# Turning attention probabilities outside TensorE in a two-layer diffusion backbone: VectorE 32x32 blocks and a round trip through DRAM

## The chip, the cores and the metric

The kernel runs on one core of one Trainium2 chip. The metric is the device time of one execution in microseconds. The kernel before took 809.46 us (median of 3 runs, 809.27 to 809.84). A difference of less than about 0.2% can't be told from no change.

A core has TensorE (PE in the profile; PEld are its weight loads), VectorE (DVE), ScalarE (ACT), GpSimd (POOL) and SyncE (SP), which here only issues DMAs.

## The reference

512 latent tokens and 256 context tokens of width 1024 pass two layers. Layer 0 is differential attention (8 heads, each with two score maps over head width 64), layer 1 grouped-query attention (8 query heads of width 128 on 2 key/value heads). Latent queries read all 768 keys, context queries (layer 0 only) read the 256 context keys.

```python
h = rms_norm(x, pre_g[i]) * (1 + scale) + shift        # scale, shift, gate from adaLN of c
q, k, v, z = split(h @ w_in)                           # layer 1: q, k also RMS-normed; then rotary
s = einsum('bqhgd,bkhd->bhgqk', q, k) * Dh ** -0.5
p = softmax(s, axis=-1)
o = einsum('bhgqk,bkhd->bqhgd', p, v)
# layer 0:  o = o1 - lam * o2, rms_norm(o, subln_g) * (1 - lam_init)
y = (o * silu(z)) @ w_out
x = x + gate * rms_norm(y, post_g[i])
```

Everything is float32; the kernel splits each operand of a large product in a rounded part and a rest (`hi` and `lo`) and adds three products (`mm3`: hi·hi, hi·lo, lo·hi).

## The kernel before

Tokens stand in tiles of 128. In layer 0 the kernel goes head by head; a head has three chunks: chunk 0 and 1 are two query tiles each of latent tokens (256 queries against 768 keys), chunk 2 the two query tiles of context. Layer 1 has 8 heads with two chunks of two latent query tiles. A **pair** is such a chunk of 256 latent queries of one head: 16 in layer 0, 16 in layer 1, 32 in all.

A pair passes these steps. One score unit for each of its two query tiles (`s_units`, `s1_units`): TensorE writes scores into the PSUM tile `sc`, VectorE takes the row maximum (`tensor_reduce`), ScalarE the exponential into `p`, GpSimd scales `p` by the reciprocal sum; in layer 0 VectorE then subtracts the second map (`scalar_tensor_tensor`). Now `p` holds queries on partitions, but the product with v needs keys on partitions. So a `tstep` for each 256 keys lets TensorE transpose four 128x128 blocks into a PSUM bank (12 transposes in a pair), ScalarE copies them, rounded, to `ah`, VectorE forms the rest `al`. An `mstep` then multiplies with v: six matmuls of 256 columns, 18 in a pair (tiles `bk<-ah,vh` and the like).

Between these steps TensorE does the projections (q, k, v, the gate z) and the output products of the layer; those that aren't due are "fill". Weights come by one queue: SP loads a 512 KB block into `raw` (2 buffers), ScalarE rounds it to `whi`, GpSimd or VectorE forms `wlo`; 3 or 4 such pairs of tiles are held.

The order of all instructions on every engine, SP's DMA issues too, is fixed when the program is built: class `Plan` records each operation with a price and a priority, `Plan.schedule` lays them out in time with these prices, and the result is written to the engines in this order. An engine works in that order and waits at each instruction for what it needs; whatever stands behind it on this engine waits too. The lines of all these operations are one line of the profile (L395 before, L411 after), so tiles are told apart by name.

Of the kernel before, what the change touches and what calls it, by code (L numbers as in the profile page):

```python
# [15 lines left out]
P = 128  # L16
# [31 lines left out]
WBUFS = 3  # L48
XE = [2, 2, 2, 2, 3, 3]
# [24 lines left out]
AB = 3  # L74
MEM = 227168
AHEAD_OPS = 1500
MARGIN = 1.08
SLOT = {}
# [28 lines left out]
class Plan:  # L107


    def __init__(self, mem, psum, sizes):  # L110
        self.mem, self.sizes = mem, sizes
# [10 lines left out]
    def pool(self, name, side="left", psum=False):  # L122
        return Pool(self, name, side, psum)

# [41 lines left out]
    def add(self, q, meth, args, kw):  # L166
# [14 lines left out]
        for aps_, w in ((ins, 0), (outs, 1)):  # L181
            for ap in aps_:
                if ap.space == bass.MemoryType.DRAM:
                    continue
                name, spans, parts = self.places(ap)
                if name not in self.banks:
# [103 lines left out]
    def schedule(self, rank):  # L290
# [15 lines left out]
        while len(order) < count:  # L306
# [79 lines left out]
class Emit:  # L386
# [7 lines left out]
    def add(self, eng, meth, args, kw):  # L394
        self.ops.append(getattr(eng, meth)(*args, **kw))  # L395
        return self.ops[-1]

# [81 lines left out]
def tile_backbone(  # L479
# [30 lines left out]
    ps1 = ctx.enter_context(pl.pool("ps1", psum=True))  # L510

# [24 lines left out]

    def mm3(o, ahi, alo, bhi, blo, start, stop):
# [4 lines left out]
    def pv_mm(o, vh, vl, c, ah, al, kt, first, last):  # L542
        terms = [(v, a, e) for v, a in ((vh, ah), (vl, ah), (vh, al)) for e in range(2)]
        for i, (v, a, e) in enumerate(terms):
            nc.tensor.matmul(o, v[:, kt + e, c], a[:, e * 256:e * 256 + 256], start=first and i == 0, stop=last and i == 5)
# [492 lines left out]
    def v_mm(o, w, t, k_lo=0, k_hi=KT, first=True, last=True):  # L1038
        for kt in range(k_lo, k_hi):
            sl = slice(t * P, (t + 1) * P)  # L1040
# [82 lines left out]
    with pl.pool("t0") as t0:  # L1123
# [58 lines left out]
        def qk_split_(h, rr, eng=nc.gpsimd):  # L1182
            qk[h] = tuple(t0.tile([P, T], F32R, tag=f"qk{i}", name=nm("qk"), bufs=1) for i in range(4))
            for r, hi, lo in ((rr[0], *qk[h][:2]), (rr[1], *qk[h][2:])):
# [79 lines left out]
        def s_units(h, qts):  # L1264
            res = []

            def unit(qt):
# [11 lines left out]
                prev = None  # L1279
                for j in range(nk // w):  # L1280
                    c = slice(k0 + j * w, k0 + j * w + w)
                    for i, (a, b) in enumerate(((qh, kh_), (qh, kl_), (ql, kh_))):
                        for m in (1, 0):
                            r = slice(m * 64, m * 64 + 64)
                            with after(prev), chained(prev):
                                prev = nc.tensor.matmul(
                                    sc[m][:, j if nk == T else m, :w], a[r, tok], b[r, c], start=i == 0, stop=i == 2)
                for m in range(2):
# [3 lines left out]
                    pt = t0.tile([P, T], F32, tag=f"p{m}", name=nm("p"), bufs=6 if m == 0 else 2)[:, :nk]  # L1292
# [827 lines left out]
```

## Time and profile before

| | before |
|---|---|
| median of 3 runs | 809.46 us |
| the profiled execution: its own time | 808.79 us |
| its span | 807.0 us |
| mean granted TensorE clock | 0.993 |
| busy: PE / PEld | 786.4 us (97%) / 699.8 us (87%) |
| busy: DVE / ACT / POOL | 473.6 (59%) / 482.0 (60%) / 437.4 us (54%) |
| moved by DMA | 77.78 MB, mean 96 GB/s |

The span is the time from the first to the last instruction. A matmul's busy time runs longer than the step from one matmul to the next, since matmuls are pipelined; where the rate of TensorE matters, the starts of neighbours are to be read. The DMA columns of a window are the mean busy share of the core's 16 DMA engines and the rate in GB/s.

### The profile page before, as it was taken

What the parts mean: (1) busy time and instruction counts of PE and PEld (TensorE: products, weight loads), DVE (VectorE), ACT (ScalarE), POOL (GpSimd) and SP (SyncE); (2) the same over time, 40 slices, a digit from 0 to 9 for tenths busy, and PEclk for the clock granted to TensorE, in tenths of its full rate; (3) what the DMA queues carried; (4) which work ended last, traced back from release to release, by engine and by line L of the source; (5) the groups of instructions that cost most, each with busy time, mean ns of one, the idle gap of its engine ahead of it and who ended that gap; (6) DMA issues with size and microseconds to landing.
All of it is one profiled execution on the core that took longest, in us unless ns stands there. A gap on an engine that the chain in (4) does not pass through costs nothing.

```text
span 807.0 us, 14385 instructions
## 1 busy us (share of the span) xinstructions
PE 786.4 (97%) x5482; PEld 699.8 (87%) x5482; DVE 473.6 (59%) x824; ACT 482.0 (60%) x1083; POOL 437.4 (54%) x512
## 2 busy tenths in 40 slices
PE   7899999999999999999999999999999999999997
PEld 5779888889887898797989998898999899898886
DVE  3425787774847546656546743788346455655625
ACT  5524577684565645666538843784466676768622
POOL 4545776874585654757923312366887646644101
PEclk9899999999999999999999999999999999999999
DMA  9951120132142431323430152035321200201112
GB/s 302 363 180 67 65 75 31 40 108 89 40 158 79 144 105 53 105 80 96 165 106 27 62 227 79 1 89 175 120 70 53 96 11 27 79 27 55 51 53 105
DMA packets 41541, 77.78 MB, mean 96 GB/s; under 512 B 3584, under 2 KB 18688, under 8 KB 41472
## 3 DMA queue, kind: packets, MB, share of 16 engines
q1 hardware_dynamic: 38048, 71.71, 27.4%
q10 hardware_dynamic: 3424, 5.15, 1.8%
q8 instruction: 43, 0.70, 0.4%
q14 instruction: 26, 0.21, 0.1%
HBM read 70.56 MB, written 2.10 MB: 90 GB/s over the span
## 4 chain that ended last, share of the span: by engine, by line
PE 91%; DVE 3%; ACT 2%; DMA 2%; issue 1%; SPq 0%; POOL 0%; ACTq 0%; DVEq 0%; POOLq 0%
PE bk L395 75%; PE sc L395 16%; DMA ag<-in_ada_w 1%; DMA raw<-in_post_g 1%; DVE gacc L395 1%; DMA gw<-in_ada_w 0%; ACT whi L395 0%; SPq L395 0%; DVE h L395 0%; ACT sq L395 0%; DVE hf L395 0%; ACT p L395 0%; DVE sw L395 0%; DVE gate L395 0%; ACT jk L395 0%
## 5 line engine op out<-in xcount | busy, mean ns | idle before, releaser
L395 PE MATMUL bk<-whi,h 128*128 128x256 f32 (+1 forms) x1184 | 244.6, 299 | 2.0 <-DVE kn L395 1.3
L395 PE MATMUL bk<-h,whi 128*128 128x512 f32 (+2 forms) x832 | 225.6, 351 | 0.0
L395 POOL TENSOR_TENSOR wlo<-raw,whi 128x256 fp32r<-128x256 f32 x200 | 162.5, 839 | 76.7 <-ACT whi L395 75.3
L395 PEld LDWEIGHTS bk<-whi,h 128*128 128x128 f32 x1184 | 191.0, 189 | 14.6 <-issue 4.9
L395 PE MATMUL bk<-wlo,h 128*128 128x256 f32 (+1 forms) x592 | 176.5, 299 | 0.0
L395 PEld LDWEIGHTS bk<-h,whi 128*128 128x128 f32 x832 | 144.1, 188 | 16.5 <-issue 4.4
L395 PE MATMUL bk<-h,wlo 128*128 128x512 f32 (+2 forms) x416 | 145.7, 351 | 0.0
L395 DVE TENSOR_REDUCE sm<-sc 128x1 f32<-128x768 f32 (+2 forms) x114 | 101.0, 897 | 25.7 <-PE sc L395 25.4
L395 PEld LDWEIGHTS bk<-wlo,h 128*128 128x128 f32 x592 | 111.7, 189 | 4.8 <-issue 1.4
L395 POOL TENSOR_SCALAR p<-p,sm 128x768 f32<-128x768 f32 (+1 forms) x80 | 68.4, 858 | 77.6 <-DVE sm L395 72.8
L395 DVE TENSOR_TENSOR al<-bk,ah 128x512 fp32r<-128x512 f32 x104 | 69.4, 685 | 39.3 <-ACT ah L395 38.8
L395 ACT CAST whi<-raw 128x1024 fp32r<-128x1024 f32 (+1 forms) x70 | 71.7, 1026 | 31.9 <-PE bk L395 27.7
L395 ACT ACTIVATE p<-sc,sm 128x768 f32<-128x768 f32 (+1 forms) x96 | 72.9, 762 | 21.6 <-DVE sm L395 15.6
L395 ACT CAST ah<-bk 128x512 fp32r<-128x512 f32 x104 | 59.0, 590 | 43.5 <-PE bk L395 43.1
L395 PEld LDWEIGHTS bk<-h,wlo 128*128 128x128 f32 x416 | 78.4, 188 | 7.5 <-issue 1.3
L395 PE MATMUL bk<-ident,p 128*128 128x128 f32 x416 | 64.3, 275 | 1.6 <-DVE ql L395 1.1
L395 PEld LDWEIGHTS bk<-ident,p 128*128 128x128 f32 x416 | 49.0, 141 | 11.4 <-issue 2.0
L395 DVE SCALAR_TENSOR_TENSOR p<-p,sm,p 128x768 f32<-128x768 f32 (+1 forms) x48 | 53.4, 1120 | 3.3 <-POOL p L395 0.5
L395 ACT ACTIVATE jk<-bk 128x128 f32<-128x128 f32 (+4 forms) x66 | 22.7, 345 | 53.5 <-PE bk L395 34.4
L395 POOL TENSOR_TENSOR sz<-sz,za 128x384 f32<-128x384 f32 (+1 forms) x24 | 29.4, 1227 | 40.3 <-ACT za L395 39.7
L395 PE MATMUL sc<-qk,qk 64*128 64x384 f32 (+1 forms) x480 | 50.6, 341 | 0.0
L395 DVE RECIPROCAL sm<-sm 128x1 f32<-128x1 f32 (+1 forms) x114 | 18.1, 159 | 52.0 <-ACT p L395 51.5
(191 smaller groups left out, 1375.5 us busy)
## 6 DMA issues: line engine op xcount, KB each, us to landing
raw<-in_a_w SPq DMA_DIRECT2D x30, 512.0 KB, 3.5
araw<-in_ada_w SPq DMA_DIRECT2D x12, 1024.0 KB, 5.3
raw<-in_b_w SPq DMA_DIRECT2D x20, 512.0 KB, 3.5
ag<-in_ada_w SPq DMA_DIRECT2D x32, 256.0 KB, 6.5
raw<-in_w_out SPq DMA_DIRECT2D x16, 512.0 KB, 3.6
sw<-qr ACTq DMA_DIRECT2D x32, 128.0 KB, 2.1
gw<-in_ada_w SPq DMA_DIRECT2D x8, 512.0 KB, 4.1
xt<-in_x SPq DMA_DIRECT2D x4, 512.0 KB, 5.1
```

The costliest lines, as they stand in the source:

```text
L395: self.ops.append(getattr(eng, meth)(*args, **kw))
```

## The change

A pair's latent probabilities are no longer transposed by TensorE. The exponentials of both query tiles go into one tile `pp` of 24 x 2 x 32 columns: 24 blocks of 32 keys, and in each the two query tiles side by side. When both are scaled, `turn` lets VectorE transpose all 32x32 blocks of `pp` in place in one instruction (128 x 1536). SP then stores `pp` to two DRAM scratch tiles `dr` (64 partitions of 1536 floats each, 384 KB) and reads them back with four loads of 192 KB into `at` (128 partitions x 4 x 384). Store and loads stand in SP's one queue; a load waits for the landing of its half store. ScalarE and VectorE split `ah` and `al` straight from `at` in SBUF instead of from a PSUM bank. The 32 transposes of the context chunks stay on TensorE.

The blocks come back with the keys in another order, so this order is given to keys and values: the score products read permuted k tiles (`ordered`, `k_tr`), and the v projections read their 128 tokens of h with a step of 4 tokens (latent tiles) or 2 (context tiles) as TensorE's weights (`keys`). The buffers of `ah` and `al` go from 3 to 2 (`AB`), the six (layer 0) or five (layer 1) single `p` tiles give way to two `pp` and two `at`. In the plan every DMA is taken to land 1000 ns later (`DPAD`), and SP's issue is priced at 450 ns instead of 330; so the order on all engines is laid out anew.

```diff
+DPAD = 1000
...
-AB = 3
...
+AB = 2
+P0B = 2
+ATB = 2
+PPB = 2
+DRSPLIT = 2
+DRB = 6
+PEWAY = ((), ())
...
-                go = s + (330 if e == "SP" else 450)
+                go = s + 450
                 dma = max(dma, go + 300) + op.cost / 350.0
-                end = max(go + 1700 + op.cost / 350.0, dma) + (800 if op.cost == 131072 else 300)
+                end = max(go + 1700 + op.cost / 350.0, dma) + (800 if op.cost == 131072 else 300) + DPAD
...
+    def keys(src, t):
+        if t < NQ:
+            return src[:, :S].rearrange("p (x k) -> p k x", k=4)[:, t]
+        return src[:, S:].rearrange("p (x k) -> p k x", k=2)[:, t - NQ]
...
+    def by_k(ap, n):
+        return by_a(ap, 192)[:, :, P:].rearrange("p a (k j) -> p k a j", k=2) if n == 2 else ap.rearrange("p (a k j) -> p k a j", a=4, k=6)
...
+    def turn(pool, pp):
+        flat = pp.rearrange("p b u x -> p (b u x)")
+        nc.vector.transpose(flat, flat)
+        at = pool.tile([P, 4, 384], F32, tag="at", name=nm("at"), bufs=ATB)
+        for lo in range(0, 4, 4 // DRSPLIT):
+            n = 4 // DRSPLIT
+            dr = drp.tile([P // DRSPLIT, 4 * 384], F32, tag="dr", name=nm("dr"), bufs=DRB)
+            nc.sync.dma_start(dr[:, :], flat[32 * lo:32 * (lo + n), :])
+            for q in range(n):
+                nc.sync.dma_start(at[:, lo + q, :], dr[32 * q:32 * q + 32, :].rearrange("j (a c) -> a j c", a=4))
+        return at
 
...
+    def split_at(ah, al, src, moved):
+        hi, lo = (by_a(ah, P), by_a(al, P)) if moved else (ah, al)
+        nc.scalar.copy(hi, src)
+        nc.vector.tensor_tensor(lo, src, f32(hi), ALU.subtract)
+
+    def unit_view(pp, u):
+        return pp[:, :, u, :]
...
-            mm3(o, hhi[kt][:, sl], hlo[kt][:, sl], wh[:, c], wl[:, c], first and kt == 0, last and kt == KT - 1)
+            mm3(o, keys(hhi[kt], t), keys(hlo[kt], t), wh[:, c], wl[:, c], first and kt == 0, last and kt == KT - 1)
...
+            nc.scalar.copy(qk[h][0], rr[0])
+            eng.tensor_tensor(qk[h][1], rr[0], f32(qk[h][0]), ALU.subtract)
+            for lo_, hi_, k in ((0, S, 4), (S, T, 2)):
+                (hi, r), (lo, _) = (ordered(t, rr[1][:, lo_:hi_], lo_, k) for t in qk[h][2:])
...
+                            if moved:
+                                b_ = b[r, j * w:j * w + w]
...
+                    if moved and m == 0:
+                        pt = unit_view(pair[qt // 2], qt % 2)
+                        pv_ = pt.rearrange("p (j b) x -> p j b x", j=2)
+                        src = scv.rearrange("p j (b x) -> p j b x", x=32)
...
-                        res.append(ps_[0])
+                        if not moved:
+                            res.append(ps_[0])
+                        elif qt % 2:
+                            res.append(turn(t0, pair[qt // 2]))
...
             def tstep(kt):
-                tr = trp()
-                for e in range(2):
-                    j = kt + e - kts[0]
-                    for i, a in enumerate(at):
-                        nc.tensor.transpose(tr[:, e * 256 + i * P:e * 256 + (i + 1) * P], a[:, j * P:(j + 1) * P], ident)
+                if not moved:
+                    tr = trp()
+                    for e in range(2):
+                        for i, a in enumerate(at):
+                            src = a[:, (kt + e - kts[0]) * P:(kt + e - kts[0] + 1) * P]
+                            nc.tensor.transpose(tr[:, e * 256 + i * P:e * 256 + (i + 1) * P], src, ident)
                 if h == 0 and ch == 0 and kt == 0:
                     t0.tile([P, 8], F32, name="pad_a")
                 ah = t0.tile([P, 512], F32R, tag="ah", name=nm("ah"), bufs=AB)
                 al = t0.tile([P, 512], F32R, tag="al", name=nm("al"), bufs=AB)
-                nc.scalar.copy(ah, tr)
-                nc.vector.tensor_tensor(al, tr, f32(ah), ALU.subtract)
+                split_at(ah, al, at[0][:, :, kt * 64:kt * 64 + P] if moved else tr, moved)
...
-            mm3(o, h1hi[:, kt, sl], h1lo[:, kt, sl], wh[:, c], wl[:, c], kt == 0, kt == KT - 1)
+            a, b = (keys(t_[:, kt, :], t) if perm else t_[:, kt, sl] for t_ in (h1hi, h1lo))
+            mm3(o, a, b, wh[:, c], wl[:, c], kt == 0, kt == KT - 1)
...
+            kd = [t.rearrange("p g (a n) -> p g a n", a=4) for t in (kh, kl)]
+            k = 4 if m < NQ else 2
+            for b in range(1 if m < NQ else 2):
+                a, c = (m, slice(0, P)) if m < NQ else (2 * (m - NQ) + b, slice(P, 192))
+                hi, lo = (t[:, :, a, c].rearrange("p g (k j) -> p g k j", k=k) for t in kd)
+                src = tv[:, :, b * 64:b * 64 + 32 * k].rearrange("p g (j k) -> p g k j", k=k)
...
+                if not moved:
+                    res.append(pt)
+                elif m % 2:
+                    res.append(turn(t1q, pair[0]))
```

Three places show the new order. The names: `sc` are score tiles, `kh`, `kl` keys, `qh`, `ql` queries, `h` the normed tokens, `whi` and `wlo` weights, `bk` PSUM banks.

SP's queue in the middle of layer 1, before: weight blocks and two rows of parameters follow each other.

```order
L395 DMA raw_7243<-in_b_w 128x1024
L395 DMA raw_7252<-in_b_w 128x1024
L395 DMA raw_7409<-in_ada_b 128x512
L395 DMA raw_7409<-in_post_g 128x512
L395 DMA raw_7425<-in_b_w 128x1024
L395 DMA raw_7622<-in_b_w 128x1024
```

SP's queue there after: ahead of the rows of parameters stand the two half stores and the four loads of two pairs.

```order
L411 DMA raw_7229<-in_b_w 128x1024
L411 DMA dr_7112<-pp_7066 64x1536
L411 DMA dr_7116<-pp_7066 64x1536
L411 DMA at_7111<-dr_7112 128x1x384 x2
L411 DMA at_7111<-dr_7116 128x1x384 x2
L411 DMA dr_7264<-pp_7191 64x1536
L411 DMA dr_7268<-pp_7191 64x1536
L411 DMA at_7263<-dr_7264 128x1x384 x2
L411 DMA at_7263<-dr_7268 128x1x384 x2
L411 DMA raw_7377<-in_ada_b 128x512
```

Twelve DMAs have come in between a weight block and the parameters; each load waits for a store that stands ahead of it in the same queue, and what stands behind the load waits too.

TensorE in layer 1, before: the end of a `tstep`'s four transposes and the rows behind them (`p` are the probabilities of one query tile).

```order
L395 MATMUL bk_70<-ident,p_7745 128x128
L395 MATMUL bk_70<-ident,p_7677 128x128
L395 MATMUL bk_70<-ident,p_7745 128x128
L395 MATMUL sc_72<-kh,ql_7568 128x384
L395 MATMUL sc_72<-kh,qh_7567 128x384
L395 MATMUL sc_72<-kl,qh_7567 128x384
L395 MATMUL sc_72<-kh,ql_7568 128x384
L395 MATMUL bk_71<-wlo_7246,h_689_5300 128x256
L395 MATMUL bk_71<-whi_7245,h_690_5301 128x256
```

TensorE in layer 1 after, at one pair's product with v: a projection (`bk<-whi,h`) runs up to it.

```order
L411 MATMUL bk_71<-wlo_7232,h_721_5270 128x256
L411 MATMUL bk_71<-whi_7231,h_722_5271 128x256
L411 MATMUL bk_70<-ah_7551,vh 128x256 x2
L411 MATMUL bk_70<-ah_7551,vl 128x256 x2
L411 MATMUL bk_70<-al_7552,vh 128x256 x2
L411 MATMUL bk_70<-ah_7587,vh 128x256 x2
L411 MATMUL bk_70<-ah_7587,vl 128x256 x2
L411 MATMUL sc_74<-kh,qh_7520 128x384
L411 MATMUL sc_74<-kl,qh_7520 128x384
L411 MATMUL bk_70<-al_7588,vh 128x256 x2
L411 MATMUL bk_70<-ah_7640,vh 128x256 x2
L411 MATMUL bk_70<-ah_7640,vl 128x256 x2
```

The transposes, which stood between score products and the product with v, have gone from TensorE; the product now needs `ah` and `al` that are made from `at`, and the three steps of a pair follow closely on each other.

VectorE in layer 1, before: row maxima, the rotary products of the next queries (`ta`, `tb`), and the rests `al` read from a bank.

```order
L395 TENSOR_REDUCE sm_7006<-sc_72 128x1
L395 TENSOR_TENSOR ta_6988<-bk_68,ropeb 128x256
L395 TENSOR_TENSOR al_7020<-bk_69,ah_7019 128x512
L395 TENSOR_TENSOR al_7046<-bk_70,ah_7045 128x512
L395 TENSOR_TENSOR tb_6989<-bk_68,ropeb 128x2x64 x2
```

VectorE there after: the block transpose stands between row maxima and rests, which are read from `at`.

```order
L411 TENSOR_REDUCE sm_7102<-sc_74 128x1
L411 TENSOR_TENSOR ta_7034<-bk_72,ropeb 128x256
L411 TENSOR_TENSOR al_6955<-at_6824,ah_6954 128x512
L411 TENSOR_TENSOR al_7004<-at_6824,ah_7003 128x512
L411 RECIPROCAL sm_7106<-sm_7106 128x1
L411 TENSOR_REDUCE sm_7187<-sc_75 128x1
L411 TENSOR_TENSOR al_7053<-at_6824,ah_7052 128x512
L411 STREAM_TRANSPOSE pp_7066<-pp_7066 128x1536
L411 TENSOR_REDUCE sm_7254<-sc_74 128x1
```

VectorE carries one more instruction in a pair, and the maxima of later units stand behind the rests of an earlier pair.

More of the change, by code (lines that the diff above doesn't have):

```diff
@@ L182, in add @@
             for ap in aps_:
-                if ap.space == bass.MemoryType.DRAM:
+                far = ap.space == bass.MemoryType.DRAM
+                if far and all(ap.tensor.name != d.tensor.name for d in self.drams):
                     continue
-                name, spans, parts = self.places(ap)
-                if name not in self.banks:
+                name, spans, parts = (ap.tensor.name, [(0, 2048)], 1) if far else self.places(ap)
+                if name not in self.banks and not far:
                     at = spans[0][0]
@@ L1264, in s_units @@
         def s_units(h, qts):
-            res = []
+            res, pair = [], {}
             def unit(qt):
@@ L1773, in tile_backbone @@
                 o = pj(256)
-                run(proj_tok(o, wk if what == "k" else wv, m))
+                run(proj_tok(o, wk if what == "k" else wv, m, what == "v"))
                 if late:
@@ L1849, in s1_units @@
         def s1_units(h, ms):
-            res = []
+            res, pair = [], {}
+            moved = dma_way(1, h, ms[0] // 2)
             def unit(m):
@@ L1877, in pv1_steps @@
             st = {}
+            moved = dma_way(1, h, ch)
             def tstep(kt):
-                tr = trp()
-                for e in range(2):
-                    for i, a in enumerate(at):
-                        nc.tensor.transpose(tr[:, e * 256 + i * P:e * 256 + (i + 1) * P], a[:, (kt + e) * P:(kt + e + 1) * P], ident)
+                if not moved:
+                    tr = trp()
+                    for e in range(2):
+                        for i, a in enumerate(at):
+                            src = a[:, (kt + e) * P:(kt + e + 1) * P]
+                            nc.tensor.transpose(tr[:, e * 256 + i * P:e * 256 + (i + 1) * P], src, ident)
                 if h == 0 and ch == 0 and kt == 0:
```

119 lines of the change are left out of this document (84 added, 35 removed).

## Prediction

> **What bounds the kernel now.** I read the page's busy times and its chain first, then the windows of both attention stages, the groups by form, TensorE's timeline, and the DMA rows.
>
> ```profile
> span 807.0 us, 14385 instructions
> PE 786.4 (97%) x5482; PEld 699.8 (87%) x5482; DVE 473.6 (59%) x824; ACT 482.0 (60%) x1083; POOL 437.4 (54%) x512
> PE 91%; DVE 3%; ACT 2%; DMA 2%; issue 1%; SPq 0%; POOL 0%; ACTq 0%; DVEq 0%; POOLq 0%
> ```
>
> TensorE is the bound: the chain that ended last runs over it for 91%. The other engines have some 40% to spare as a mean, which says little about a stage, so here are layer 1's attention (587 to 762 us; its first score product and its last product with v are in the next rows), layer 0's, and five microseconds at the start, where the DMA engines are full (columns: PE, PEld, DVE, ACT, POOL busy, clock, DMA share, GB/s).
>
> ```profile
> 587.00:762.00 175.00, 171.43 (x1197) 160.77 (x1196) 97.08 (x181) 122.16 (x277) 98.12 (x124) 1.00 0.17 52
> 170.00:470.00 300.00, 298.06 (x2135) 261.86 (x2134) 181.63 (x293) 185.21 (x391) 169.60 (x167) 1.00 0.30 96
> 5.00:10.00 5.00, 2.50 (x22) 2.19 (x20) 0.72 (x5) 4.34 (x8) 2.66 (x6) 1.00 1.07 374
> L395 PE MATMUL sc<-kh,qh x64: 333/338/445, 587.0 to 728.3; 128*128 128x384 f32 x64
> L395 PE MATMUL bk<-al,vh x96: 277/280/367, 609.8 to 761.2; 128*128 128x256 f32 x96
> ```
>
> TensorE has no hole in either. DVE is at 55% and ACT at 70% of layer 1's stage, and DMA is nearly idle in it (0.17).
>
> **What leaves TensorE.** 32 pairs times 12 make 384 of the 416 transposes. What one costs is read from the starts of neighbours:
>
> ```profile
> L395 PE MATMUL bk<-ident,p 128*128 128x128 f32 x416 | 64.3, 275 | 1.6 <-DVE ql L395 1.1 <-DVE al L395 0.4
> 639.99 0.60 PE L395 MATMUL bk<-ident,p 128*128 128x128 f32 x4
> 640.34 0.48 PE L395 MATMUL bk<-h,whi 128*128 128x512 f32 x1
> 640.66 0.40 PE L395 MATMUL bk<-ah,vh 128*128 128x256 f32 x2
> ...
> 646.17 0.39 PE L395 MATMUL bk<-h,wlo 128*128 128x512 f32 x1
> 646.40 0.39 PE L395 MATMUL bk<-h,whi 128*128 128x512 f32 x1
> ```
>
> Four start at 639.99 and the next matmul at 640.34: 0.35 us. That matmul then takes 0.32 us to its successor, where the same shape undisturbed takes 0.23 (646.17 to 646.40); so four cost 0.35 + 0.09 = 0.44, or 0.11 us each. 384 x 0.11 = 42.2 us leave the path, half of it (21.1) from each layer. Were nothing else to change, the profiled execution (808.8 us of its own, span 807.0) would take 766.6.
>
> **What VectorE and ScalarE get.**
>
> ```profile
> L395 DVE TENSOR_REDUCE sm<-sc 128x1 f32<-128x768 f32 x96 | 90.3, 949 | 24.9 <-PE sc L395 24.6
> L395 DVE TENSOR_TENSOR al<-bk,ah 128x512 fp32r<-128x512 f32 x104 | 69.4, 685 | 39.3 <-ACT ah L395 38.8
> L395 DVE SCALAR_TENSOR_TENSOR p<-p,sm,p 128x768 f32<-128x768 f32 x32 | 41.8, 1307 | 2.3
> L395 DVE TENSOR_TENSOR h<-hf,h 128x512 fp32r<-128x512 f32 x20 | 15.7, 791 | 4.6 <-ACT h L395 4.0 <-POOL hf L395 0.6
> L395 ACT ACTIVATE p<-sc,sm,qrs 128x768 f32<-128x768 f32 x32 | 31.8, 994 | 2.6 <-PE bk L395 1.4
> L395 POOL TENSOR_SCALAR p<-p,sm 128x768 f32<-128x768 f32 x64 | 59.4, 930 | 71.9 <-DVE sm L395 67.2 <-PE bk L395 4.5
> L395 DVE TENSOR_SCALAR xt<-xt,sm 128x1024 f32<-128x1024 f32 x5 | 4.2, 843 | 11.2 <-POOL sm L395 11.1
> L395 ACT CAST ah<-bk 128x512 fp32r<-128x512 f32 x104 | 59.0, 590 | 43.5 <-PE bk L395 43.1 <-ACT p L395 0.2
> L395 ACT CAST h<-hf 128x512 fp32r<-128x512 f32 x12 | 7.3, 619 | 0.0
> ```
>
> No block transpose stands in this trace. Its 1536 columns cost between 1.3 us (843 ns for 1024, the fastest wide row) and 2.6 us (1307 for 768, the slowest). I take 1.8: from 685 for 512 and 949 for 768, which is 1.03 ns a column over some 0.16. In layer 1 that is 16 x 1.8 = 29 us more, and `al` from two SBUF tiles costs up to 48 x 0.11 = 5 (791 against 685). DVE would hold 97 + 34 = 131 of a stage of 175 - 21 = 154 us, 85%; at the high end 144, 94%. It stays below the bound. ACT's `ah` from SBUF is 0.03 us dearer (619 against 590), 1.4 us in layer 1: 124 of 154. I put these at nothing, covered by that idle time; if it isn't there, the high end shows as waits of `al`. The K split in two instructions (one more on ACT and on POOL in each head of layer 0), the 24 x 32 views of `pp` that ACT, POOL and DVE work on, and the rearranged head copies go the same way: POOL, at 98 of 175 and 170 of 300 us, has the most room.
>
> **Weight loads with a step.** The v products read h with a step of 4 tokens as TensorE's weights: 4 latent tiles x 8 x 3 for each of four head pairs in layer 0 and once in layer 1, 480 loads (context tiles have a step of 2).
>
> ```profile
> L395 PEld LDWEIGHTS bk<-h,whi 128*128 128x128 f32 x832 | 144.1, 188 | 16.5 <-issue 4.4
> L395 PEld LDWEIGHTS bk<-ident,p 128*128 128x128 f32 x416 | 49.0, 141 | 11.4 <-issue 2.0 <-DVE ql L395 1.5 <-DVE vlo L395 1.0
> 640.89 0.40 PE L395 MATMUL bk<-ah,vl 128*128 128x256 f32 x2
> 641.13 0.40 PE L395 MATMUL bk<-al,vh 128*128 128x256 f32 x2
> ...
> 642.53 0.34 PE L395 MATMUL sc<-kh,qh 128*128 128x384 f32 x1
> 642.70 0.34 PE L395 MATMUL sc<-kl,qh 128*128 128x384 f32 x1
> ```
>
> All loads in the trace are contiguous. From 640.66 to 641.13 four matmuls of 256 columns start, 0.118 us each (one of 384 takes 0.17). The transposes, of half as many columns, still take 0.11, so a load needs up to 0.11, nearly all that the matmul hides. A load at half speed would need 0.22 and cost 0.102 x 480 = 49 us. I take 0, as the contiguous rows, which are the nearest, and keep 49 as the other end.
>
> [...]
>
> **The way through DRAM.** Per pair two half stores of 64 x 1536 x 4 = 393 KB and four loads of 128 x 384 x 4 = 197 KB, each way 786 KB.
>
> ```profile
> q1 hardware_dynamic: 38048, 71.71, 27.4%
> q10 hardware_dynamic: 3424, 5.15, 1.8%
> q1 hardware_dynamic: 4016, 8.91, 16.1%
> sw<-qr ACTq DMA_DIRECT2D x32, 128.0 KB, 2.1
> out_x<-u SPq DMA_DIRECT2D x6, 256.0 KB, 2.1
> raw<-in_b_w SPq DMA_DIRECT2D x20, 512.0 KB, 3.5
> L395 SPq DMA_DIRECT2D raw<-in_b_w x20: 327/328/407, 492.3 to 697.0; - x20
> ```
>
> The first two rows give what a busy DMA engine moves: 71.71 MB in 27.4% of 16 x 807 us is 20.3 KB/us, 5.15 MB in 1.8% is 22.2; the full window gave 374 / 16 = 23.4. The third row is layer 1's window: 8.91 MB of weights.
>
> How many of the 16 engines a load runs on is the unknown that decides. Every transfer of this trace has 128 or 64 partitions as the outer step on both sides. The new loads don't: the source, `j (a c) -> a j c`, has 4 as its outer step, the target 128. At the one end they spread over all 16 engines, a load lands after some 2.3 us (128 KB in 2.1, 512 KB in 3.5), and engines and stage don't notice. At the other they run on 4, the largest cut that both outer steps allow, and always the same 4, as equal work for one queue would. I take 4: no row has such a source, and a transfer cut by its outer step can't be cut in more.
>
> [...]
>
> On 4 engines, one pair puts on each of them 786 / 4 = 197 KB of loads, 786 / 16 = 49 of stores, and 8.91 MB / 16 pairs / 16 = 35 of weights: 281 KB. At 22.2 KB/us that is 12.6 us a pair (12.0 at 23.4, 13.8 at 20.3). TensorE's pair in layer 1 is 154 / 16 = 9.6. So in layer 1 DMA takes over as the bound: 16 x 12.6 = 202 us, and about 13 that it can't overlap: ahead of the first load a second score unit, maximum, exponential, scaling, block transpose and store (some 1 us each, the store nearer 3), behind the last `ah`, `al` and 18 matmuls (0.6 + 0.7 + 2.1). Stage 215 instead of 154: +61 us. Layer 0's products with v run from 102.9 to 465.3:
>
> ```profile
> L395 PE MATMUL bk<-ah,vhi x112: 277/280/683, 102.9 to 465.3; 128*128 128x256 f32 x112
> ```
>
> That is 22.7 us a pair, 21.3 without the transposes, and a pair with its share of weights (96 GB/s) is 197 + 49 + 128 = 374 KB or 16.8 us. It fits, so layer 0 gets nothing more: fill hides it, and where fill lacks, up to some 10 us of waits would show.
>
> Sum: 808.8 - 42.2 + 61 = 827.6 for the profiled execution. The median of the runs before lies 0.7 above its profile, so **828 us**. Its own range is 808.8 - 42.2 + (192 or 221, + 13, - 154) = 818 to 847, and with a softer start and end of the stage 812 to 850.
>
> What queues behind the waits: a load holds SP's queue until its half store has landed, and weight blocks stand behind it (328 ns an issue, six issues 2 us); ACT's `whi` and then TensorE wait for those. The product with v comes late next, and with it `pp` and the exponentials of the pair after the next.
>
> **Rivals.**
>
> *Loads spread over all engines: faster.* A pair then has 786 x 2 / 16 + 35 = 133 KB an engine, 6 us, below TensorE's 9.6. The turn (block transpose 1.8, store about 3.2 and load about 2.3 with their issues 1.5, some 9 us) lies under TensorE's own work: in the new order the least cover of a pair, from its last score product to its first product with v, is 83 matmuls of 256 columns, 30 of 384 and 4 transposes, 83 x 0.118 + 30 x 0.17 + 4 x 0.11 = 15.3 us, against some 4 for maximum, exponential and scaling, the 9, and 1.3 for the split. Tight, so 5 us of waits: 766.6 + 5 + 0.7 = 772 (765 to 785). For it: all transfers seen are fast. Against: the source's pattern is unlike them.
>
> *Four engines, but each faster than any row shows.* At 29 KB/us a pair needs 9.7 us; the stage grows only by the 13 and some waits: 785 to 807, still faster. The point where it decides is a stage of 154 + 42 = 196 us, or 11.4 us a pair, 24.6 KB/us; the fullest window reached 23.4.
>
> *Weight loads at half speed, turn hidden: slower.* 772 + 49 = 821. Above 78 ns more for each load the gain is gone (37.5 / 480). For it: only 8 ns of cover. Against: nothing measured.
>
> *No difference:* the DMA stage costs just what the transposes gave.
>
> **Chances.** Loads on four engines and slower 0.53; spread wide 0.27; four engines but faster 0.09; stepped weight loads decide 0.08; within 0.2%, which is what the measurement can tell from no change, 0.03. So faster 0.36, same 0.03, slower 0.61. The range that leaves out no more than 2 in 10 reaches from the spread case to the long DMA stage: 768 to 850.
>
> **What would show it.** Right: landing times of `at<-dr` of 5 us and more against about 2 of the small rows; TensorE idle ahead of products with v in layer 1, ACT `ah` waiting for DMA; layer 1's stage over 200 us; layer 0 shorter by some 20. Wrong: loads that land in 2 to 3 us, a TensorE still without holes (the spread case), or v products with starts 0.2 apart (the stepped loads). DVE's block transpose above 2.6 us would upset the cover.

## The result, and the profile after

The changed kernel takes **959.13 us** (median of 4 runs, 957.22 to 961.92) against 809.37 (809.26 to 809.84) for the kernel before on the same chip: 1.185 times as long, 95% interval 1.181 to 1.189. The forecast was 828, with a range up to 850: slower was right, the size was not. The first lines of the page after, its row of the granted clock and its chain of waits:

```profile
span 959.2 us, 14097 instructions
...
PE 842.7 (88%) x5098; PEld 747.8 (78%) x5098; DVE 520.9 (54%) x859; ACT 485.3 (51%) x1093; POOL 442.5 (46%) x519
...
PEclk9999989899998999799898999999998978789899
...
PE 37%; DMA 21%; ACT 4%; POOL 3%; issue 3%; SPq 3%; DVE 2%; ACTq 0%; DVEq 0%; POOLq 0%
```

The transposes are gone (5482 matmuls have become 5098), and yet TensorE is busy 842.7 us instead of 786.4. Its idle time went from 20.6 to 116.5 us (span less busy), and DMA holds 21% of the chain, where it held 2%. So two things want an explanation: holes, and matmuls that take longer. Where they lie is read from the same stages in both kernels, cut at the first score product of layer 0, the first product with layer 0's `w_out`, the first transpose of layer 1's input, its first score product and its last product with v. First before, then after (PE, PEld, DVE, ACT, POOL busy, clock, DMA share, GB/s):

```profile
0.00:79.90 79.90, 72.59 (x479) 57.84 (x479) 34.21 (x72) 37.90 (x66) 40.91 (x57) 0.94 0.69 228
79.90:453.10 373.20, 371.25 (x2623) 323.23 (x2622) 239.82 (x389) 232.70 (x490) 229.86 (x225) 1.00 0.26 85
505.00:587.00 82.00, 79.73 (x566) 73.48 (x565) 56.05 (x116) 48.80 (x150) 51.39 (x69) 1.00 0.32 99
587.00:761.20 174.20, 170.63 (x1191) 159.97 (x1190) 96.38 (x179) 121.71 (x276) 98.12 (x124) 1.00 0.17 52
```

```profile
0.00:88.90 88.90, 81.85 (x483) 67.40 (x483) 31.68 (x73) 38.76 (x68) 37.86 (x57) 0.98 0.63 206
88.90:526.60 437.70, 400.57 (x2424) 349.65 (x2424) 265.20 (x406) 233.55 (x497) 235.67 (x233) 0.94 0.43 130
578.70:671.80 93.10, 89.59 (x559) 83.66 (x558) 54.95 (x119) 49.89 (x152) 47.83 (x67) 0.98 0.26 81
671.80:916.90 245.10, 181.81 (x1037) 165.55 (x1036) 123.59 (x197) 123.47 (x277) 102.59 (x127) 0.87 0.47 142
```

| stage | before | after | difference |
|---|---|---|---|
| start | 79.9 | 88.9 | +9.0 |
| layer 0's attention and fill | 373.2 | 437.7 | +64.5 |
| layer 0's last projection | 51.9 | 52.1 | +0.2 |
| layer 1's k and v | 82.0 | 93.1 | +11.1 |
| layer 1's attention and fill | 174.2 | 245.1 | +70.9 |
| tail | 45.8 | 42.3 | -3.5 |

More than half of the loss lies in layer 0 and in stages with no turn at all, where the forecast had a gain of 21 and nothing.

**The loads run on four engines.** The DMA rows of 9.5 us in layer 1, in 40 slices (busy share in tenths, and GB/s). Two stores go out in the middle; the rest is one pair's loads:

```profile
DMA  1222222232222293959595799986421221222322
GB/s 45 103 103 97 97 97 103 97 91 71 71 97 103 103 388 116 362 149 362 149 336 175 259 356 310 323 304 235 104 32 32 78 84 71 103 110 103 123 103 103
```

In the slices of the loads the share is between two and three tenths at 97 to 103 GB/s: four of 16 engines, 25 KB/us on each, the number that the prediction took. The timeline of SP's queue shows what follows:

```profile
720.08 2.38 SPq L411 DMA_DIRECT2D at<-dr  x4
724.13 1.14 SPq L411 DMA_DIRECT2D dr<-pp  x2
732.36 1.18 SPq L411 DMA_DIRECT2D at<-dr  x2
```

The stores of 724.13 move in the full slices, 725 to 729 us, but the next loads can be issued only at 732.36. The DMA packets of 728.8 to 730.2 us and of 730.6 to 732.3 us say what lies between (a load's packets have 1536 bytes, a store's 6144: 61 of the first make the 0.09 MB of one window, 8 of the first and 27 of the second nearly all of the 0.18 MB of the other):

```profile
DMA packets 63, 0.09 MB, mean 67 GB/s; under 512 B 2, under 2 KB 63, under 8 KB 63
```

```profile
DMA packets 43, 0.18 MB, mean 105 GB/s; under 512 B 8, under 2 KB 16, under 8 KB 43
q1 hardware_dynamic: 43, 0.18, 25.5%
```

First come loads alone, and then, on a quarter of the engines, what is left of the stores. So part of each store goes over the four engines of the loads, behind the loads of the pair before; load and store take turns there, and from one group of loads to the next it is 12.3 us here (11.8 to 15.1 in the stage, and once 22.6). ACT's `ah` waits for the landing (101.8 us in all), VectorE's `al` for `ah` (114.9), and TensorE for both (67.2 and 3.7). Waits in the whole kernel, SP's queue first:

```profile
SPq L411 <- DMA dr<-pp: 129.5, 30, 9.3
```

```profile
ACT ah L411 <- DMA at<-dr: 101.8, 22, 7.5
```

The chain of waits in the same microseconds, and TensorE's timeline:

```profile
721.91 9.45 DMA at<-dr
...
731.45 1.15 ACT ah L411 x2
...
734.19 10.34 DMA at<-dr
```

```profile
718.59 0.79 PE L411 MATMUL bk<-ah,vh 128*128 128x256 f32 x2 [2.37 <-ACT ah L411]
...
721.31 0.62 PE L411 MATMUL bk<-ah,vl 128*128 128x256 f32 x2
721.74 0.42 PE L411 MATMUL bk<-h,whi 128*128 128x512 f32 x1
722.00 0.40 PE L411 MATMUL bk<-al,vh 128*128 128x256 f32 x2
722.23 0.40 PE L411 MATMUL bk<-ah,vh 128*128 128x256 f32 x2
...
732.12 0.80 PE L411 MATMUL bk<-ah,vh 128*128 128x256 f32 x2 [7.49 <-ACT ah L411]
732.72 0.63 PE L411 MATMUL bk<-ah,vl 128*128 128x256 f32 x2
```

The timeline shows a second cost of a hole. After 7.49 us without work two matmuls of 256 columns take 0.60 us from start to start (732.12 to 732.72); at 721.31, still in the shadow of the hole that ended at 718.59, 0.43, and from 722.00 on 0.23. The page's clock row has 7s and 8s where these holes lie; in layer 1 the granted clock is 0.87 of 245 us, 32 us not granted, in layer 0 0.94 of 438, 26 us. Before the change it was 1.00 in both. Behind the hole of 2.37 us that ended at 718.59, the granted clock is 0.50 until 721.70 (0.43 us for two matmuls against 0.23), and from 732.12 to 733.00 it is 0.50 again. Of the 18 holes of 2 us or more from 60 us on, 17 are followed by 1.5 us at a granted clock of 0.78 or less, 12 of them at 0.50; the one of 3.22 us that ended at 819.40 is followed by 0.96. What decides this was not shown.

**The stepped weight loads are slow.** The group of weight loads with h among the groups by form, before and then after:

```profile
L395 PEld LDWEIGHTS bk<-whi,h 128*128 128x128 f32 x1184 | 191.0, 189 | 14.6 <-issue 4.9 <-DVE kn L395 1.6 <-DVE kl L395 0.8
```

```profile
L411 PEld LDWEIGHTS bk<-whi,h 128*128 128x128 f32 x1184 | 233.3, 229 | 15.2 <-issue 5.1 <-DVE tb L411 1.7 <-DVE kl L411 0.8
```

TensorE's timeline where a latent tile of layer 1's v projection ends and a context tile starts:

```profile
637.82 0.40 PE L411 MATMUL bk<-whi,h 128*128 128x256 f32 x1
638.05 0.40 PE L411 MATMUL bk<-wlo,h 128*128 128x256 f32 x1
638.28 0.51 PE L411 MATMUL bk<-whi,h 128*128 128x256 f32 x2
638.63 0.28 PE L411 MATMUL bk<-wlo,h 128*128 128x256 f32 x1
638.75 0.40 PE L411 MATMUL bk<-whi,h 128*128 128x256 f32 x2
```

With a step of 4 tokens the starts are 0.23 us apart (637.82, 638.05, 638.28), with 2 tokens 0.12 (638.63, 638.75), at full clock.

**VectorE's block transpose** was taken at 1.8 us and `al` at 0.11 more; both came so (`al` had 685 ns before). Their groups by form:

```profile
L411 DVE STREAM_TRANSPOSE pp<-pp 128x1536 f32<-128x1536 f32 x32 | 56.6, 1769 | 1.0 <-POOL pp L411 1.0
L411 DVE TENSOR_TENSOR al<-at,ah 128x512 fp32r<-128x512 f32 x96 | 74.4, 792 | 129.9 <-ACT ah L411 113.6 <-PE bk L411 14.5 <-DMA araw<-in_ada_w 1.5
```

### The profile page after: what moved, and what is told of

It reads as the page before. It is cut to its first block, busy times and chain, and to the rows that moved or that the text cites. A ratio compares the mean times of both kernels' runs of the same rounds, so it can differ in the third digit from the quotient of the medians.

```text
span 959.2 us, 14097 instructions
## 1 busy us (share of the span) xinstructions
PE 842.7 (88%) x5098; PEld 747.8 (78%) x5098; DVE 520.9 (54%) x859; ACT 485.3 (51%) x1093; POOL 442.5 (46%) x519
## 4 chain that ended last, share of the span: by engine, by line
PE 37%; DMA 21%; ACT 4%; POOL 3%; issue 3%; SPq 3%; DVE 2%; ACTq 0%; DVEq 0%; POOLq 0%
PE bk L411 32%; DMA at<-dr 15%; PE sc L411 5%; DMA dr<-pp 4%; SPq L411 3%; ACT ah L411 2%; DMA araw<-in_ada_w 1%; DVE pp L411 1%; POOL wlo L411 1%; DVE sm L411 0%; POOL qk L411 0%; ACT p L411 0%; ACT whi L411 0%; ACT pp L411 0%; POOL pp L411 0%
## 5 line engine op out<-in xcount | busy, mean ns | idle before, releaser
L411 PE MATMUL bk<-whi,h 128*128 128x256 f32 (+1 forms) x1184 | 288.7, 332 | 2.3 <-DVE tb L411 1.4
L411 PEld LDWEIGHTS bk<-whi,h 128*128 128x128 f32 x1184 | 233.3, 229 | 15.2 <-issue 5.1
L411 POOL TENSOR_TENSOR wlo<-raw,whi 128x256 fp32r<-128x256 f32 x200 | 159.9, 823 | 88.9 <-ACT whi L411 88.5
L411 DVE TENSOR_TENSOR al<-at,ah 128x512 fp32r<-128x512 f32 x96 | 74.4, 792 | 129.9 <-ACT ah L411 113.6
L411 PEld LDWEIGHTS bk<-wlo,h 128*128 128x128 f32 x592 | 135.3, 229 | 6.7 <-POOL wlo L411 1.8
L411 POOL TENSOR_SCALAR pp<-pp,sm 128x768 f32<-128x768 f32 x64 | 63.0, 984 | 143.8 <-DVE sm L411 142.3
L411 ACT CAST ah<-at 128x512 fp32r<-128x512 f32 x96 | 57.5, 616 | 129.6 <-DMA at<-dr 101.8
L411 DVE TENSOR_REDUCE sm<-sc 128x1 f32<-128x768 f32 (+2 forms) x114 | 101.3, 895 | 23.4 <-PE sc L411 23.2
L411 ACT CAST whi<-raw 128x1024 fp32r<-128x1024 f32 (+1 forms) x70 | 71.4, 1021 | 40.4 <-PE bk L411 21.5
L411 PE MATMUL bk<-ah,vh 128*128 128x256 f32 x96 | 27.5, 379 | 56.7 <-ACT ah L411 56.7
L411 DVE STREAM_TRANSPOSE pp<-pp 128x1536 f32<-128x1536 f32 x32 | 56.6, 1769 | 1.0 <-POOL pp L411 1.0
L411 PEld LDWEIGHTS sc<-qk,qk 64*128 64x128 f32 x480 | 39.8, 191 | 13.3 <-issue 4.2
L411 POOL TENSOR_TENSOR qk<-qr,qk 128x768 fp32r<-128x768 f32 (+2 forms) x21 | 31.6, 1516 | 38.4 <-ACT qk L411 34.7
```

## The experiments

### Undoing each part of the change

Loads on all engines. The four pieces of a row are sent to their places by the store instead of by the load; a quarter is stored by itself, so that the outer step is 32, and the loads become plain rows of 128 partitions. Bytes, queue and count of transfers (six a pair) stay.

```diff
-            dr = drp.tile([P // DRSPLIT, 4 * 384], F32, tag="dr", name=nm("dr"), bufs=DRB)
-            nc.sync.dma_start(dr[:, :], flat[32 * lo:32 * (lo + n), :])
+            dr = drp.tile([P, n * 384], F32, tag="dr", name=nm("dr"), bufs=DRB)
             for q in range(n):
-                nc.sync.dma_start(at[:, lo + q, :], dr[32 * q:32 * q + 32, :].rearrange("j (a c) -> a j c", a=4))
+                to = dr[:, q * 384:q * 384 + 384].rearrange("(a j) c -> j a c", a=4)
+                nc.sync.dma_start(to, flat[32 * (lo + q):32 * (lo + q) + 32, :].rearrange("j (a c) -> j a c", a=4))
+            nc.sync.dma_start(at[:, lo:lo + n, :], dr.rearrange("p (q c) -> p q c", q=n))
```

> Same bytes by the same queue, six transfers a pair as before, but every one cut in 32 or 128 rows at its outer step on both sides: each quarter of the turned pair is stored by itself with the four pieces of a row sent to their places, and a half is loaded as 128 plain rows. Theory (loads on four of 16 engines make the holes): TensorE's idle time falls from 116 us to under 40, the clock returns to near 1, and what is left over the kernel before is the stepped weight loads: 809 - 42 + 46 = 813, with up to 15 us of waits 812 to 830. Rival (the holes come from the turn's own chain, store, landing, load, landing in SP's order, whatever the engines): the holes stay, above 900.

Contiguous weight loads. Key tile k holds tokens 128k to 128k + 127 (step 1) instead of every fourth token; k is stored to match, and the kernel computes the same.

```diff
     def keys(src, t):
-        if t < NQ:
-            return src[:, :S].rearrange("p (x k) -> p k x", k=4)[:, t]
-        return src[:, S:].rearrange("p (x k) -> p k x", k=2)[:, t - NQ]
+        return src[:, t * P:(t + 1) * P]
...
-        return a.rearrange("p a (k j) -> p a k j", k=k), r.rearrange("p (a j k) -> p a k j", a=4, k=k)
+        return a.rearrange("p a (k j) -> p a k j", k=k), r.rearrange("p (k a j) -> p a k j", a=4, k=k)
...
+            hi, lo = (t[:, :, :, m * 32:(m + 1) * 32] for t in kd)
+            src = tv.rearrange("p g (a j) -> p g a j", a=4)
```

> The key order is changed so that key tile k holds tokens 128k to 128k+127: the products of v read h without a step, the loads through DRAM stay on four engines. Theory (a weight load with a step of 4 floats costs 0.095 us more at its start-to-start time, 480 of them): every weight load back at 0.19 us; some 17 us come back in the start and in layer 1's projections, where nothing else limits, and up to 29 in layer 0 as far as TensorE isn't waiting for DMA there: 912 to 942. Rival (the loads are slow because the DMA engines write SBUF at the same time): they stay at 0.33 us, and the time at 959.

Both edits:

> Both edits together. Theory: both costs go and the transposes' 42 us stay saved: 767 to 785, faster than the kernel before. Rival (the turn's chain): above 850.

Measured, the changed kernel against 809.37 as above and the three others against 808.03 for the kernel before on their chip (ratios with their intervals):

| | loads on 4 engines | loads on 16 engines |
|---|---|---|
| weights with a step of 4 | 959.13, 1.185 (1.181 to 1.189) | 858.52, 1.062 (1.059 to 1.066) |
| weights contiguous | 929.73, 1.149 (1.145 to 1.152) | 798.94, 0.988 (0.986 to 0.991) |

Spread loads win 100.6 us on the changed kernel, contiguous weights 29.4, both 160.2: the kernel is then faster than the one before. The rivals (the turn's own chain above 900; slow weights because of DMA traffic) are out. The first edit missed its range by 29 us and the third by 14. TensorE's idle time fell to 40.4 and 38.9 us (span less busy: 854.4 less 814.0, 796.3 less 757.4), so nearly to the 40 that the first was to have at most; but that is still 20 and 18 us more than before the change, the granted clock came back to 0.979 and 0.978 where it had been 0.993, and in the first the steps, put at 46 us, cost 59.6. The costs cover each other: the slow weight loads cost 59.6 us with loads on 16 engines and 29.4 with four, where TensorE would have stood still for part of that time anyway.

In the kernel with both edits, the windows of the two attention stages, a row of its waits and one of its DMA issues (KB each, median us to landing):

```profile
80.80:446.10 365.30, 355.59 (x2425) 307.04 (x2425) 271.80 (x406) 231.26 (x497) 239.61 (x233) 0.98 0.49 155
581.30:762.80 181.50, 169.43 (x1089) 153.75 (x1089) 135.76 (x200) 126.25 (x283) 112.57 (x128) 0.99 0.63 195
```

```profile
ACT ah L411 <- DMA at<-dr: 5.7, 5, 2.1
```

```profile
at<-dr SPq DMA_DIRECT2D x64, 384.0 KB, 3.7
```

Twice the bytes of a load now land in 3.7 us where the chain showed 9.5 to 10.3 (for these bytes alone four engines at 25 KB/us would need 3.9), and `ah` waits 5.7 us in all instead of 101.8. Against the contiguous kernel on four engines, layer 0 falls from 424.1 to 365.3 us and layer 1 from 241.6 to 181.5. The windows of that kernel:

```profile
80.90:505.00 424.10, 374.49 (x2425) 321.89 (x2425) 267.60 (x406) 230.08 (x497) 234.38 (x233) 0.93 0.45 134
639.60:881.20 241.60, 181.44 (x1035) 164.90 (x1035) 123.59 (x196) 123.20 (x276) 100.34 (x126) 0.85 0.48 144
```

So the four engines cost layer 0 as much (59 us) as layer 1 (60). The DMA rows of the kernel with both edits from 614.5 to 619 us, in which it issues two loads and three stores:

```profile
DMA packets 505, 1.01 MB, mean 224 GB/s; under 512 B 47, under 2 KB 308, under 8 KB 505
q1 hardware_dynamic: 505, 1.01, 89.4%
```

There 89.4% of the 16 engines are busy. The edit changes the packets too (stores from 6144 to 1536 bytes, loads from 1536 to 3072; 261 and 197 of these make the 1.01 MB), and the order, which is laid out anew with other sizes; that the engines' number counts, and not the packets', rests on the DMA rows above, where each of the four is full at 25 KB/us.

### The weight loads by themselves

The kernel before, with v's products reading h in steps and nothing else moved; the order of the instructions on every engine stays that of before.

```diff
-            mm3(o, hhi[kt][:, sl], hlo[kt][:, sl], wh[:, c], wl[:, c], first and kt == 0, last and kt == KT - 1)
+            mm3(o, keys(hhi[kt], t), keys(hlo[kt], t), wh[:, c], wl[:, c], first and kt == 0, last and kt == KT - 1)
```

> The kernel before with one thing added: the products of v read h with a step of 4 (latent) or 2 tokens (context), nothing else moved; v's tokens then no longer match the probabilities' order, so this kernel computes another attention. Theory: 480 loads of step 4 at 0.33 us, 240 of step 2 at 0.19; 809 + 46 = 855 (850 to 860). Rival (slow only beside the DMA traffic of the turns): 809 to 815.

861.09 us, 1.065 (1.062 to 1.067): 53.1 us for 480 loads, 0.11 each, 1 us above the range, with TensorE busy 98% and no turn anywhere. The stages, to be set beside those of before:

```profile
0.00:87.80 87.80, 81.31 (x479) 67.54 (x479) 32.75 (x72) 37.76 (x66) 38.11 (x57) 0.98 0.63 207
87.80:494.70 406.90, 404.69 (x2623) 356.65 (x2622) 238.89 (x389) 232.71 (x490) 230.06 (x225) 1.00 0.24 78
546.70:638.60 91.90, 90.88 (x567) 84.70 (x565) 54.25 (x116) 48.69 (x150) 50.71 (x69) 1.00 0.28 88
```

Start +7.9, layer 0 +33.7, layer 1's k and v +9.9. That is nearly all of what the changed kernel lost in its start (9.0) and in layer 1's k and v (11.1).

The same with a step of 2 for the latent tiles too:

```diff
         if t < NQ:
-            return src[:, :S].rearrange("p (x k) -> p k x", k=4)[:, t]
+            return src[:, t // 2 * C:t // 2 * C + C].rearrange("p (x k) -> p k x", k=2)[:, t % 2]
```

> The kernel before with all six token tiles of v's products read with a step of 2 tokens (8 bytes) and none with 4; as in the kernel with step 4 alone, v's order no longer matches the probabilities, so another attention is computed. [...] Rival (the cost grows with the step): a third or half of the 53 us for each load, 720 of them: 835 or more.

808.51 us against 806.94, 1.0022 (1.0008 to 1.0035): 1.6 us for 720 loads, next to nothing. The cost does not grow evenly with the step: it is next to nothing at 8 bytes and 0.11 us a load at 16; other steps weren't run. Load and matmul of 256 columns together go from 0.118 to 0.23 us at 16 bytes and stay at 0.12 at 8.

### Holes: bytes, or an order made for short landings

The planner alone is changed, for the kernel with contiguous weights and loads on four engines; it reckons with 7 or 10 us more until a load has landed; `ah`, `al` and the products with v then stand later in their queues.

```diff
-                end = max(go + 1700 + op.cost / 350.0, dma) + (800 if op.cost == 131072 else 300) + DPAD
+                end = max(go + 1700 + op.cost / 350.0, dma) + (800 if op.cost == 131072 else 300) + (DPAD + 7000 if op.cost == 196608 else DPAD)
```

> The kernel with contiguous weight loads and the loads still on four engines; the planner alone is changed: it takes a load of a quarter to land 7 us later than it did (it took 3.6 us from issue, the trace of the changed kernel shows some 10.5). Theory (the holes come from an order made for short landings: ACT's queue stands in front of `ah` with exponentials and weight splits behind it): ACT's waits for these loads fall from 99 us to under 35, layer 0's attention goes from 424 to about 375, and layer 1's to what four engines need, 281 KB a pair at 25 KB/us, 11.2 us, 180 + 13 = 193 instead of 241: 930 - 49 - 48 = 833 (820 to 870). Rival (the four engines are themselves the limit in both layers): the waits stay, above 905.

> The same with 10 us instead of 7. Theory: within 15 us of the 7 us plan, on either side, as the waits that are left are those of layer 1. Rival (bytes): above 905.

877.73 us (1.086, 1.083 to 1.090) and 869.20 (1.077, 1.073 to 1.080) instead of 929.73: the order was worth 52 to 61 us. It was more than the rival allowed and less than the theory had it (the first run is 8 us above its range, the second inside the 15 us). The windows of the two attention stages with 10 us, and TensorE's waits for `ah`, first with contiguous weights alone and then with 10 us:

```profile
78.90:468.30 389.40, 362.37 (x2407) 310.64 (x2406) 266.19 (x401) 228.30 (x491) 236.76 (x232) 0.95 0.48 145
607.20:832.90 225.70, 185.93 (x1088) 165.97 (x1087) 132.81 (x200) 128.09 (x283) 106.17 (x127) 0.93 0.52 154
```

```profile
PE bk L411 <- ACT ah L411: 64.5, 18, 8.4
```

```profile
PE bk L411 <- ACT ah L411: 9.8, 6, 3.8
```

Layer 0 gets back 35 of its 59 us, and TensorE's waits for `ah` fall from 64.5 to 9.8. Layer 1 gets back 16 (and 10 in the tail, to which less is left over); 44 us against 16 engines stay there. To see whether these are bytes, every second pair of layer 1, and then all of them, went back to TensorE:

```diff
-PEWAY = ((), ())
+PEWAY = ((), ((0, 1), (1, 1), (2, 1), (3, 1), (4, 1), (5, 1), (6, 1), (7, 1)))
```

> Loads on four engines, contiguous weight loads, loads planned 10 us later (869.2), with every second pair of layer 1 turned by TensorE again. Theory (in layer 1 the bytes on four engines are the limit): two pairs then put 197 + 2 x 49 / 2 + 2 x 35 = 316 KB on each of them, 12.6 us at 25 KB/us, against some 20 us of TensorE's: hidden, layer 1 falls from 226 to about 182 us and the time to 825 (815 to 835). Rival (each turn costs a wait of its own, the bytes don't matter): half of the 44 us stays, 847 (841 to 855).

> The same with all of layer 1 turned by TensorE. Theory: layer 1 as in the kernel before, layer 0 still with its waits on four engines (389 us against 361 on 16): 869 - 45 = 824 (816 to 832), so level with the half above. Rival (a wait for each turn): 20 below the half.

857.90 us (1.058, 1.053 to 1.064) with half of layer 1's turns, 829.99 (1.026, 1.023 to 1.029) with none. Half the turns keep 28 of some 40 us. My theory, that the bytes on four engines are the limit in layer 1, gave 825 for half the turns and falls for this kernel, though 829.99 lies in its range for none (816 to 832); the rival gave 847 for half the turns and is 11 too low. The windows of layer 1's stage, with half of its turns and then with none:

```profile
610.40:811.10 200.70, 176.73 (x1095) 161.54 (x1094) 115.01 (x188) 124.53 (x277) 99.66 (x126) 0.91 0.37 108
```

```profile
607.30:781.00 173.70, 171.09 (x1185) 159.74 (x1184) 97.05 (x179) 122.61 (x276) 99.41 (x125) 1.00 0.16 52
```

With eight turns the DMA share is down to 0.37 and layer 1 still 27 us longer, with idle time (24 us) and clock that was not granted (0.91 of 201, 18 us, some of it inside the holes). So a cost stays that the bytes don't explain. That each slow turn has its price at its own place is not shown: of the 24 us, TensorE's waits for `ah` in this stage are 8.7, and the others stand at other tiles (`gate`, `tb`, `al`, `pp`). Why eight turns cost 3.5 us each and sixteen 2.5 wasn't settled either.

### What is left in the kernel with both edits

The planner is told 1.5 and 3 us more for its loads:

```diff
-                end = max(go + 1700 + op.cost / 350.0, dma) + (800 if op.cost == 131072 else 300) + DPAD
+                end = max(go + 1700 + op.cost / 350.0, dma) + (800 if op.cost == 131072 else 300) + (DPAD + 1500 if op.cost == 393216 else DPAD)
```

> The kernel with both edits (loads on 16 engines, contiguous weight loads), with a planner that takes each of its loads to land 1.5 us later. Theory: the 28 us that this kernel still loses against 766 (TensorE idle 44 instead of 26 us, and the half clock that follows a hole) come from turns that last 8 to 14 us and were planned at less: 785 to 795. Rival (those holes have another cause, VectorE above all): 796 to 803.

> The same with 3 us. Theory: 780 to 795, at or below the 1.5 us plan. Rival: 796 or more, as later products with v push the exponentials of later pairs back.

795.08 us (0.984, 0.982 to 0.987) and 800.09 (0.990, 0.988 to 0.992). The first is the fastest kernel of this study, 1.6% below the one before, at the edge of its range; the second belongs to the rival. A plan that is too late costs about as much as one that is too early. Last, this kernel with layer 1 turned by TensorE:

```diff
-PEWAY = ((), ())
+PEWAY = ((), ((0, 0), (0, 1), (1, 0), (1, 1), ... (7, 0), (7, 1)))
```

> The fastest version so far (loads on 16 engines, contiguous weight loads, loads planned 1.5 us later, 795.1), with layer 1's pairs turned by TensorE again; layer 0 goes through DRAM. By the windows of the 795.1 kernel layer 1 and the tail gained only 3 us on the kernel before (216.8 against 219.9) and layer 0 13: theory (layer 1's saved transposes are given back as waits): 794 to 800. Rival (each layer brings half of what the transposes took, less its waits): 806 to 814.

799.30 us (0.988, 0.985 to 0.990), as the theory had it: the turn brings layer 1 some 0.3%, 2 to 4 us, though 192 transposes left it, and the intervals of the two kernels overlap (0.982 to 0.987, 0.985 to 0.990). The window of that stage in the 795.08 kernel shows why, and below it the one with TensorE's transposes, of which 2 us are idle:

```profile
574.80:758.60 183.80, 170.84 (x1091) 155.51 (x1091) 132.77 (x200) 125.89 (x283) 111.95 (x128) 0.99 0.62 192
```

```profile
576.80:750.70 173.90, 171.66 (x1188) 160.19 (x1187) 96.42 (x179) 122.84 (x276) 100.14 (x126) 1.00 0.17 55
```

With the turn there are 13 us of idle time, and VectorE is at 133 of 184 us. The stage is ten us longer; the tail gives them back and 4 more (33.0 us against 46.8), which fits work of the tail that moved into the holes.

## Why the prediction was wrong, point by point

- **The sign and the unknown it hung on: right.** "I take 4" for the loads' engines is what the DMA rows show, and with 16 the time falls by 100.6 us. That a load runs on 4 and a half store on 16, which the sum used, no row of the kernel before shows; in the changed kernel 2 to 3 tenths of the 16 engines are busy while loads move, at 97 to 103 GB/s, and 9 tenths in slices in which stores move, at up to 388. Landings of 5 us and more, `ah` waiting for DMA, and a layer 1 above 200 us were all there.
- **"A load at half speed would need 0.22 and cost 0.102 x 480 = 49 us. I take 0": the first step that failed, by size.** Alone the steps cost 53.1 us, so the upper end was nearly the value. The rival with that cost was given a chance of 0.08. The reason, that contiguous loads are the nearest rows, was no reason: none of those rows has a step. Worse, the two unknowns were made rivals (stepped loads *with the turn hidden*), so that no case had both; their sum, 828 + 49 = 877, lies above the range.
- **"It fits, so layer 0 gets nothing more": the second.** 16.8 us of DMA in 21.3 of TensorE compares averages. Four engines cost layer 0 59 us (424.1 against 365.3), of which the planner's order was 35. A load lands some 10 us after its issue, where the plan had 3.6, and the static order has an `ah` on ACT at the time the plan believed in. What stands behind it in ACT's queue waits with it while the engines' average has room: in layer 0 at 306.67 us an `ah` starts after 3.87 us of waiting for its load, and exponentials and a weight split stand behind it. The prediction saw such waits for SP's queue, and allowed layer 0 "up to some 10 us".
- **"16 x 12.6 = 202 us, and about 13": near by luck in the middle, short at the ends.** At the 25 KB/us that the loads reached, the 281 KB of a pair are 11.2 us, not 12.6, and from one group of loads to the next it is 11.8 to 15.1 us; so waits stand where the sum had bytes. And the first `ah` of layer 1 comes 31.8 us after its first score product, where 13 were put for start and end, and over the stage a pair takes 13.9. From ACT's timeline and from the rows of the tile `at` (first and last start):

```profile
703.58 1.14 ACT L411 CAST ah<-at 128x512 fp32r<-128x512 f32 x2 [5.51 <-DMA at<-dr]
```

```profile
L411 ACT CAST ah<-at x96: 600/617/647, 121.5 to 913.5; 128x512 fp32r<-128x512 f32 x96
```

  (913.5 - 703.6 - 2) / 15 = 13.9. 31.8 + 210 + some 3 is the stage of 245 where 215 stood. With 11.2 us of bytes in 13.9 the bytes alone were not the limit in that order either, and the run with half the turns shows a cost without it.
- **The clock: a term that was missing.** The sum priced a hole at its length. Granted clocks of 0.94 and 0.87 took another 26 and 32 us in the two stages, some of it inside the holes.
- **"One busy DMA engine moves 22.2 KB/us": 25.** By the second rival's own condition (24.6) the kernel should have come out faster. The condition was met and did not decide, since it knew only of layer 1.
- **VectorE and ACT at nothing: right.** 1769 ns for the block transpose, 792 for `al`, 616 for `ah`; TensorE waited 3.7 us for `al` in all, 1.8 before.
- **"42.2 us leave the path":** not seen alone. With both costs undone and the order retuned 12.7 of them arrive. In its profiled execution the span falls by 15.4 us (807.0 to 791.6). TensorE is idle for 38.2 us (791.6 less 753.4 busy), 17.6 more than before, and its busy time falls by 33.0 (786.4 to 753.4, both at a mean clock of 0.993) where the sum had 42.2: 0.086 us for each transpose that left, not 0.11. Why the difference wasn't settled.

From 808 to 959, by the table of the two edits: 42 less for the transposes, 33 that the kernel with both edits still loses (799 against 766), 131 for four engines in place of 16 (930 against 799), 52 to 61 of them by an order that expected the loads too early, and 29 for the steps beside such loads (59.6 without them).

## What to carry to other kernels

Before a transfer is put on a critical path, look at the outer step of both its sides: 4 there meant a quarter of the engines (97 to 103 GB/s for the loads), and with the rearrangement moved from the load to the store, where the outer step was 32, 89.4% of the 16 were busy. A stationary operand read with a step of 16 bytes took load and matmul together from 0.118 to 0.23 us (256 columns), and with 8 bytes 720 loads cost 1.6 us in all; another key order, with contiguous tiles, served as well. And in a kernel with a static order the landing time that its planner believes in is part of the cost: compare latency with the cover at each place, not bytes with the average, and price a hole of TensorE at more than its length: behind 7.49 us without work two matmuls took 0.60 us here instead of 0.23.

## What was not expected of the hardware

- The four engines moved 25 KB/us each in packets of 1536 bytes (97 to 103 GB/s in sum), more than any row of the kernel before showed for a busy engine (23.4).
- Of the two half stores issued at 724.13 us most had moved by 729, at up to 388 GB/s, and the last part only some 3 us later, on a quarter of the engines (25.5%), behind another transfer's loads.
- The cost of the stepped weight load comes between a step of 8 and one of 16 bytes: 0.2% for 720 loads with 8, 6.5% for 480 with 16.
